# A hybrid state-space and attention step: reordered state-space stage, an early gated column, and queues and rooms at two stage borders

## The chip, the cores and the metric
The kernel runs on one core of a Trainium2 chip as one program. Its time is the device time of that program in microseconds: the median of three runs before is 2771.04 us (2769.51 to 2775.39).

## The reference
Two layers work on 1024 prompt tokens and 32 sample tokens of width 1024, all in float32. Layer 0 mixes by a diagonal state-space model with a gate, layer 1 by sparse attention over the 256 best keys; after each mixer stands a convolutional feed-forward unit of width 2816.

```python
def s5_mixer(u, ...):                       # 64 groups of 16 channels, 64 complex states each
    h = scan(a * h_prev + b @ u)            # over the tokens
    y = re(c @ h) + d * u
    z = gelu(y)
    g = z @ w_glu + b_glu                   # 1024 x 2048
    return g[:, :1024] * sigmoid(g[:, 1024:]), h_last

x = x + s5_mixer(rms_norm(x))               # layer 0
x = x + conv_ffn(rms_norm(x))
x = x + sparse_attention(rms_norm(x)) @ w_o # layer 1
x = x + conv_ffn(rms_norm(x))
```

## The kernel before
The program is a chain of stages: `ssm` (state-space model), `load_x` (the residual stream, transposed on chip), `glu` (the gate), `ffn(0)`, the projections and the index search, `attend`, the output projection, `ffn(1)`. The dense products write each float32 operand as a high and a low part, so that one product is three matmuls; a weight is loaded on SP's queue, ACT casts its high part (`whi`) and DVE subtracts to get the low part (`wlo`). Rooms in on-chip memory come from pools: a new tile waits until the room's former tile has been read. The layer that records the operations puts the instructions of each engine in order itself (by costs and readiness), so the order on an engine is not that of the code; the rows of the order below are what it made.

`ssm` cuts the 64 groups into eight octets `o` of 8 groups, and each octet into three subs `s` of 3, 3 and 2 groups. Tokens go in chunks of eight, 133 columns for a group: 128 of the prompt, then the state and four chunks of the sample. For an octet, `taps` and `maps` build the matrices `ix`, `cp`, `cps`, `tz` (DVE, with POOL's products `tt`, and DMAs of `kr` into `tz`). For a sub, `angles` makes the phases: POOL's `sel`, PE's matmul (L637), DVE's rounding `kk` (L639), PE again (L641 to L643), ACT's `cos` and `sin`. `states` multiplies the inputs by `inm` on PE, rotates them on DVE (`ga`, `gb`), copies the initial state into one column of `ga` (L671), scans (`en`, L673), and rotates back: POOL makes `pc` from `en` and `cos` (L678) while DVE makes `pq` from `en` and `sin` (L679). `outputs` sums three matmuls into `py` (L693 to L695), ACT copies it to `yo`. `rows(o)` regroups the octet's `yo` by eight DMAs on SP into `zo` (L702), applies gelu in place (L703), casts with a stride into `xh[o]` (L710), and subtracts with the same stride into `xl[o]` (L711). Final states `pcf`, `psf` are collected on POOL and stored from SP at the end.

Then `load_x` loads nine row tiles of x on ACT's queue (`xrow`, two rooms), transposes 72 blocks on PE (L236) and copies them to `xt`. `glu` goes over eight output columns `m`: 16 weight DMAs of 64 KB on SP (L152), two casts, two subtractions, then for each of three token blocks two sums over eight `k` (144 matmuls of 352 columns per column), sigmoid on ACT and the product on DVE. At the start of `attend` SP loads the first keys `kr`, values `vr` and queries `qr`; POOL splits the queries (`qp`), PE transposes them (L1292), ACT casts `q`, and the scores follow (L1308, L1309).

Of the kernel before, what the change touches and what calls it, by code (L numbers as in the profile page):

```python
# [9 lines left out]
F32 = mybir.dt.float32  # L10
# [3 lines left out]
ALU = mybir.AluOpType  # L14
# [27 lines left out]
MAGF = 12582912.0  # L42
RATE = 0.6
# [6 lines left out]
class Trunk:  # L50


    def __init__(self, tc, ctx, I, O):
# [9 lines left out]
        self.xh, self.xl = [], []  # L63

# [14 lines left out]
    def open_weights(self, ctx):  # L79
        self.open_psum(ctx)  # L80
        self.wr = ctx.enter_context(self.tc.tile_pool(name="wr", bufs=3, side="right", reuse_waits="tile"))
        self.wp = ctx.enter_context(self.tc.tile_pool(name="wp", bufs=4, side="right", reuse_waits="tile"))
# [12 lines left out]
    def load_vectors(self, pool):  # L95
# [13 lines left out]
        rows = [pool.tile([P, P], F32, tag="vrow", name="vrow", bufs=3) for _ in range(nt)]  # L109
        at = 0  # L110
        for name, s in srcs:
            self.voff[name] = at
            n, o = s.shape[0], 0
            while o < n:
                t, r = divmod(at, P)
                c = min(n - o, P - r)
                nc.sync.dma_start(rows[t][r : r + c, :], s[o : o + c, :])
                o += c
                at += c
        for t in range(nt):  # L120
# [10 lines left out]
    def weight(self, view, pool=False):  # L131
# [13 lines left out]
        return hi, lo  # L145

    def weight_rows(self, view, sh):

        nc = self.nc
        raw = self.wr.tile(sh, F32, tag="wraw", name="wraw")  # L150
        for k in range(sh[1]):
            nc.sync.dma_start(raw[:, k], view[:, :, k])  # L152
        hi = self.wp.tile(sh, F32R, tag="whi", name="whi")
        lo = self.wp.tile(sh, F32R, tag="wlo", name="wlo")
        nc.scalar.copy(hi, raw)
        nc.vector.tensor_sub(lo, raw, hi.bitcast(F32))
        return hi, lo
# [68 lines left out]
    def load_x(self, pool):  # L226
        nc, I = self.nc, self.I
        xp = I["x_prompt"].rearrange("b t d -> (b t) d")
        xs = I["x_sample"].rearrange("b t d -> (b t) d")
        for o, n in self.token_tiles():  # L230
            row = pool.tile([P, D], F32, tag="xrow", name="xrow", bufs=2)
            nc.scalar.dma_start(row[:n], xp[o : o + n] if o < TP else xs[:n])
            for h in range(2):
                ps = self.ps()
                for k in range(4):
                    nc.tensor.transpose(ps[:, k * P : k * P + n], row[:n, (4 * h + k) * P : (4 * h + k + 1) * P], self.ident[:n, :n])  # L236
                nc.any.tensor_copy(self.xt[:, 4 * h : 4 * h + 4, o : o + n], ps.rearrange("p (k t) -> p k t", t=P)[:, :, :n])
# [52 lines left out]
    def ssm_loads(self, tmp):  # L290
# [12 lines left out]
        xs = tmp.tile([TS + 8, D], F32, name="xs")  # L303
# [18 lines left out]
    def ssm_params(self, pool, tmp, ld):  # L322
# [132 lines left out]
        bst, bsw, ca, cb = (pool.tile([P, G, 16], F32, name=n) for n in ("bst", "bsw", "ca", "cb"))  # L455
# [31 lines left out]
    def ssm_input(self, tmp, ld):  # L487
# [9 lines left out]
        n = TS + 8  # L497
# [19 lines left out]
        room = [v[0:5, i : i + 1024].rearrange("c (j f) -> c j f", f=P) for v in ld["free"] for i in range(0, 3072, 1024)]  # L517
        for o in range(KD):
            t = self.xp.tile([5, 8, 8, 16], F32, tag="xh", name="um", bufs=KD)
# [10 lines left out]
    def ssm(self):  # L530

        nc, I, O = self.nc, self.I, self.O
        C = 133
        with ExitStack() as ctx:
            self.open_psum(ctx)
            pool = ctx.enter_context(self.tc.tile_pool(name="ssm", bufs=1, reuse_waits="tile"))
            with self.tc.tile_pool(name="ssmt", bufs=1, reuse_waits="tile") as tmp:
# [9 lines left out]
                pcf = pool.tile([P, 2, 64], F32, name="pcf")  # L547
                psf = pool.tile([P, 2, 64], F32, name="psf")
                tz = [pool.tile([P, 8, P], F32, name=f"tz{i}") for i in range(2)]
                m8s = [pool.tile([P, 8, C], F32, name=f"m8{i}") for i in range(2)]  # L550
                sels = [pool.tile([P, 400], F32R, name=f"sel{i}") for i in range(3)]
                zc = self._fill(tmp, "zc", [P, 1], 0.0)
                for t in tz:
                    nc.gpsimd.memset(t, 0.0)
                for t in m8s:
                    nc.gpsimd.memset(t[:, :, 0:1], 0.0)
                    nc.gpsimd.memset(t[:, :, 128:129], 0.0)
                for t in sels:
                    nc.vector.tensor_copy(t[:, 399:400], zc)
# [10 lines left out]
            W3 = lambda ng: ng * C + ng * C % 2  # L570
            flat = lambda v: v.rearrange("p g c -> p (g c)")

            def taps(o):
# [19 lines left out]
                for a, b in ((1, 128), (129, C)):  # L593
# [4 lines left out]
            def maps(o, d):  # L598
# [3 lines left out]
                kr = wk.tile([16, 8, P], F32, tag="kr", name="kr", bufs=1)  # L602
                for h in range(2):
# [21 lines left out]
            def angles(o, s):  # L625
# [12 lines left out]
                kk = wk.tile([P, 400], F32R, tag="kk", name="kk", bufs=2)  # L638
# [5 lines left out]
                cos = wk.tile([P, 3, C], F32, tag="cos", name="cos", bufs=3)[:, :ng]  # L644
                sin = wk.tile([P, 3, C], F32, tag="sin", name="sin", bufs=3)[:, :ng]
# [1040 lines left out]
```

## Time and profile before

| | us |
|---|---|
| median of three runs | 2771.04 |
| the profiled execution | 2771.09 |
| its span, first to last instruction | 2769.3 |
| PE busy in the span | 2576.5 (93%) |
| DVE / ACT / POOL busy | 1607.9 / 998.5 / 447.9 |

The profiled execution lies 0.05 us from the median, and 1.8 us of it lie outside the span. Over long stretches PE is busy without a gap, so the stages in which it is not are the ones to read: the state-space stage up to 254 us, the border behind it up to 286 us, the index search and projections, and the start and end of attention. Two views serve for that: the windows, which give the busy time of every engine in a stretch, and the waits, which name the instruction that waited and the one that released it.

### The profile page before, as it was taken

What the parts mean: (1) busy time and instruction counts of PE and PEld (TensorE: products, weight loads), DVE (VectorE), ACT (ScalarE), POOL (GpSimd) and SP (SyncE); (2) the same over time, 40 slices, a digit from 0 to 9 for tenths busy, and PEclk for the clock granted to TensorE, in tenths of its full rate; (3) what the DMA queues carried; (4) which work ended last, traced back from release to release, by engine and by line L of the source; (5) the groups of instructions that cost most, each with busy time, mean ns of one, the idle gap of its engine ahead of it and who ended that gap; (6) DMA issues with size and microseconds to landing.
All of it is one profiled execution on the core that took longest, in us unless ns stands there. A gap on an engine that the chain in (4) does not pass through costs nothing. (4 is left out here: it accounts for less than half of the span.)

```text
span 2769.3 us, 43229 instructions
## 1 busy us (share of the span) xinstructions
PE 2576.5 (93%) x17203; PEld 2466.9 (89%) x17203; DVE 1607.9 (58%) x3365; ACT 998.5 (36%) x2011; POOL 447.9 (16%) x696
## 2 busy tenths in 40 slices
PE   2887999999999999998898689999999999999999
PEld 2676999999999999997788667778999999999998
DVE  8886324644444444468799887663654444444443
ACT  4665213322222222225466577772322222222222
POOL 4673001100000000011245242220200000000000
PEclk9998999999999999998999799999999999999999
DMA  4334311111111111110111301202111111111111
GB/s 95 60 57 101 93 46 46 39 46 46 47 46 46 46 46 47 46 36 22 47 56 61 89 22 39 48 18 77 39 46 46 46 47 46 47 46 46 46 39 64
DMA packets 220662, 140.29 MB, mean 51 GB/s; under 512 B 50429, under 2 KB 212261, under 8 KB 220461
## 3 DMA queue, kind: packets, MB, share of 16 engines
q1 hardware_dynamic: 216733, 130.90, 17.3%
q10 hardware_dynamic: 3728, 6.64, 0.7%
q8 instruction: 135, 2.21, 0.3%
q14 instruction: 66, 0.54, 0.1%
HBM read 112.68 MB, written 13.40 MB: 46 GB/s over the span
## 5 line engine op out<-in xcount | busy, mean ns | idle before, releaser
L164 PE MATMUL ps_mm<-xh,whi 128*128 128x352 f32 x2688 | 870.3, 324 | 4.8 <-ACT whi L143 4.8
L166 PE MATMUL ps_mm<-xh,wlo 128*128 128x352 f32 x2688 | 869.5, 324 | 0.0
L165 PE MATMUL ps_mm<-xl,whi 128*128 128x352 f32 x2688 | 868.6, 323 | 0.0
L164 PEld LDWEIGHTS ps_mm<-xh,whi 128*128 128x128 f32 x2688 | 506.4, 188 | 5.1 <-ACT whi L143 5.0
L165 PEld LDWEIGHTS ps_mm<-xl,whi 128*128 128x128 f32 x2688 | 506.3, 188 | 0.0
L166 PEld LDWEIGHTS ps_mm<-xh,wlo 128*128 128x128 f32 x2688 | 506.0, 188 | 0.2 <-DVE wlo L144 0.2
L144 DVE TENSOR_TENSOR wlo<-wraw,whi 128x1024 fp32r<-128x1024 f32 (+1 forms) x145 | 175.4, 1221 | 416.7 <-ACT whi L143 416.7
L143 ACT CAST whi<-wraw 128x1024 fp32r<-128x1024 f32 (+1 forms) x145 | 149.9, 1047 | 711.9 <-PE ps_mm L165 701.8
L1559 DVE TENSOR_TENSOR xt<-xt,ps_mm 128x352 f32<-128x352 f32 x528 | 269.2, 519 | 191.6 <-PE ps_mm L166 191.5
L164 PE MATMUL ps_mm<-hh,whi 128*128 128x352 f32 x1056 | 341.1, 323 | 1.5 <-DVE xt L1559 1.5
L165 PE MATMUL ps_mm<-hl,whi 128*128 128x352 f32 x1056 | 340.9, 323 | 0.0
L166 PE MATMUL ps_mm<-hh,wlo 128*128 128x352 f32 x1056 | 340.6, 323 | 0.0
L1540 POOL COPY tails<-a 128x2 f32<-128x2 f32 x44 | 39.8, 904 | 1229.9 <-ACT a L1529 1229.9
L164 PEld LDWEIGHTS ps_mm<-hh,whi 128*128 128x128 f32 x1056 | 198.4, 188 | 2.1 <-DVE xt L1559 2.0
L166 PEld LDWEIGHTS ps_mm<-hh,wlo 128*128 128x128 f32 x1056 | 198.5, 188 | 0.0
L165 PEld LDWEIGHTS ps_mm<-hl,whi 128*128 128x128 f32 x1056 | 198.4, 188 | 0.0
L772 PE MATMUL ps_mm<-whi,xh 128*128 128x256 f32 (+3 forms) x560 | 163.6, 293 | 18.4 <-ACT raw L1173 18.4
L1547 DVE TENSOR_TENSOR c<-c,ps_mm 128x352 f32<-128x352 f32 (+2 forms) x176 | 71.5, 427 | 159.3 <-PE ps_mm L166 112.7
L773 PE MATMUL ps_mm<-wlo,xh 128*128 128x256 f32 (+3 forms) x560 | 161.9, 290 | 0.0
L774 PE MATMUL ps_mm<-whi,xl 128*128 128x256 f32 (+3 forms) x560 | 161.8, 290 | 0.0
L1529 ACT COPY a<-ps_mm 128x352 f32<-128x352 f32 (+2 forms) x176 | 61.9, 378 | 242.1 <-PE ps_mm L166 242.0
L772 PEld LDWEIGHTS ps_mm<-whi,xh 128*128 128x128 f32 (+1 forms) x560 | 104.1, 186 | 23.1 <-ACT raw L1173 21.6
(410 smaller groups left out, 3974.7 us busy)
## 6 DMA issues: line engine op xcount, KB each, us to landing
wraw<-in_ffn_w_up_dram SPq DMA_DIRECT2D x88, 512.0 KB
wraw<-in_ffn_w_down_dram SPq DMA_DIRECT2D x44, 512.0 KB
wraw<-in_ssm_w_glu_dram SPq DMA_DIRECT2D x128, 64.0 KB
wraw<-in_attn_w_in_dram SPq DMA_DIRECT2D x14, 512.0 KB
zo<-yo SPq DMA_DIRECT2D x64, 66.5 KB
xcm<-in_x_prompt_dram SPq DMA_DIRECT2D x8, 512.0 KB
cps<-cp SPq DMA_DIRECT2D x16, 256.0 KB
xrow<-in_x_prompt_dram ACTq DMA_DIRECT2D x8, 512.0 KB
```

What stands on the lines that cost most here:

```text
L143: nc.scalar.copy(hi, raw)
L144: nc.vector.tensor_sub(lo, raw, hi.bitcast(F32))
L164: nc.tensor.matmul(ps, wh, xh, start=(i == 0), stop=False)
L165: nc.tensor.matmul(ps, wh, xl, start=False, stop=False)
L166: nc.tensor.matmul(ps, wl, xh, start=False, stop=(i == n - 1))
L772: self.nc.tensor.matmul(ps, xh, hi[:, c, a:b], start=(k == 0), stop=False)
L773: self.nc.tensor.matmul(ps, xh, lo[:, c, a:b], start=False, stop=False)
L774: self.nc.tensor.matmul(ps, xl, hi[:, c, a:b], start=False, stop=(k == KD - 1))
L1529: nc.scalar.copy(u["a"][:, co + 2 : co + 2 + n], ps[:, to - b * BLK : to - b * BLK + n])
L1540: nc.gpsimd.tensor_copy(tails[:, u["f"], 0:2], u["a"][:, TP : TP + 2])
L1547: nc.vector.tensor_mul(h, h, bv[:, to - b * BLK : to - b * BLK + n])
L1559: nc.vector.tensor_add(self.xt[:, m, blocks[b]], self.xt[:, m, blocks[b]], ps[:, :BLK])
```

## The change
- State-space stage: a group has 134 columns, the sample's six first (state, four chunks, one pad), then the prompt's 128. `cos` and `sin` lie in one tile `cs`, `pc` and `pq` in one tile `pp`, and one multiplication on DVE fills both. The copy of the initial state into `ga` moves from DVE to ACT. `dgi` and the addition to `kr` move from DVE to POOL. `kk` has one room. `rows` writes gelu's result with the stride into `zt`, so that the cast and the subtraction run over 1056 adjacent columns; for the last octet half of the eight `zo` DMAs go to ACT's queue. The loads of the small vectors move from the start to the second octet; the final states are stored from POOL's queue.
- First gated column: the banks of `ssm` and of the dense stages are one pool. During the last octet `glu_first` loads both halves of column 0 (one on SP, one on POOL's queue) into rooms that have become free, with their casts and subtractions; the products for `k` 0 to 6 are issued behind the last outputs, those for `k` 7 behind them.
- `load_x` works on one column `m` (nine transposes) inside the first block of that column in `glu`, from `xcol`, two DMAs on SP.
- `glu` has its own weight rooms; column `m` loads column `m`'s weights in its turn (column 1 in that of column 0, its second half on POOL's queue). The first seven weight loads of `ffn(0)` stand on SP behind the `xcol` of column 6.
- Attention: the first keys' and queries' rooms and banks are ones that are free; `vr` and `rss` are issued behind the first two `qr`; the second keys are loaded two units later. For the output projection the two weight pools change places.

```diff
-        C = 133
+        C = 134
...
-                dgi = wk.tile([16, 8, 16], F32, tag="dgi", name="dgi", bufs=1)
-                nc.vector.tensor_mul(
-                    dgi, self.ident[:16, :16].rearrange("p (g q) -> p g q", g=1).to_broadcast([16, 8, 16]),
-                    par["dg"][:, gs].rearrange("p (g q) -> p g q", q=1).to_broadcast([16, 8, 16]))
-                nc.vector.tensor_add(kr[:, :, 0:16], kr[:, :, 0:16], dgi)
...
-                nc.vector.tensor_mul(ga, v3(p1), w["cos"])
-                nc.vector.tensor_mul(gb, v3(p2), w["sin"])
-                nc.vector.tensor_add(ga, ga, gb)
-                nc.vector.tensor_copy(ga[:, :, 128], smt[:, 33, w["gg"]])
...
+                nc.scalar.copy(ga[:, :, 0], smt[:, 33, w["gg"]])
+                gc = ga[:, :, 1:]
+                nc.vector.tensor_mul(gc, v3(p1)[:, :, 1:], w["cos"][:, :, 1:])
+                nc.vector.tensor_mul(gb[:, :, 1:], v3(p2)[:, :, 1:], w["sin"][:, :, 1:])
+                nc.vector.tensor_add(gc, gc, gb[:, :, 1:])
...
-                nc.gpsimd.memset(pc[:, :, 0:1], 0.0)
-                nc.gpsimd.memset(pq[:, :, 0:1], 0.0)
-                nc.gpsimd.tensor_mul(pc[:, :, 1:], en, w["cos"])
-                nc.vector.tensor_mul(pq[:, :, 1:], en, w["sin"])
-                for f, p in ((pcf, pc), (psf, pq)):
-                    nc.gpsimd.tensor_copy(f[:, :, w["gg"]].rearrange("p f g -> p g f"), p[:, :, 128:134:5])
+                pp = wk.tile([P, 2, 3, C + 1], F32, tag="pp", name="pp", bufs=2)[:, :, :ng]
+                pc, pq = pp[:, 0], pp[:, 1]
+                nc.gpsimd.memset(pp[:, :, :, 0:1], 0.0)
+                nc.vector.tensor_mul(pp[:, :, :, 1:], en.rearrange("p (s g) c -> p s g c", s=1).to_broadcast([P, 2, ng, C]), w["cs"])
+
+                nc.gpsimd.tensor_copy(fcs[:, :, :, w["gg"]].rearrange("p s f g -> p s g f"), pp[:, :, :, 5 : C + 1 : C - 5])
...
-                nc.scalar.activation(zo, zo, AF.Gelu_apprx_tanh)
...
-                    nc.scalar.copy(hi, src)
-                    nc.vector.tensor_sub(lo, src, hi.bitcast(F32))
+                    e = nc.scalar if last and i % 2 else nc.sync
+                    e.dma_start(zo[:, i, :], yo[o][16 * i : 16 * i + 16])
...
+                x = wk.tile([P, T], F32, tag="zt", name="zt", bufs=1)
+                for t0, t1, c0 in ((0, TP, 6), (TP, T, 1)):
+                    nc.scalar.activation(
+                        x[:, t0:t1].rearrange("p (c i) -> p i c", i=8), zo[:, :, c0 : c0 + (t1 - t0) // 8], AF.Gelu_apprx_tanh)
+                nc.scalar.copy(xh, x)
+                nc.vector.tensor_sub(xl, x, xh.bitcast(F32))
...
+                        if o == KD - 2:
+                            first = self.glu_first(pool, wk)
...
+                nc.gpsimd.dma_start(O["ssm_re_" + nm][0, 0], fin[64 * f : 64 * f + 64, 0:64])
+                nc.gpsimd.dma_start(O["ssm_im_" + nm][0, 0], fin[64 * f : 64 * f + 64, 64:128])
...
+        raw, hi, lo = (new(i) for i in range(3))
+        for k in range(KD):
+            (e or nc.sync).dma_start(raw[:, k], w[:, :, k, c : c + P])
+        nc.scalar.copy(hi, raw)
+        nc.vector.tensor_sub(lo, raw, hi.bitcast(F32))
+        return hi, lo
...
+        ws = [self.glu_weight(new(half), 0, half, nc.gpsimd if half else None) for half in range(2)]
+
+        def products():
+            self.first = [[self.ps()[:, :BLK] for _ in ws] for _ in range(NB)]
+            for ks in (range(KD - 1), (KD - 1,)):
+                for b in range(NB):
+                    for ps, w in zip(self.first[b], ws):
+                        self.glu_part(ps, w, b, ks)
+
+        return products
+
...
+                return self.glu_weight(tile, m, half, nc.gpsimd if m == 1 and half else None)
+
+            def residual(m):
+                raw = gp.tile([P, 9, P], F32, tag="xcol", name="xcol")
+                nc.sync.dma_start(raw[:, 0:8], xp[:, :, m * P : (m + 1) * P])
+                self.loaded = nc.sync.dma_start(raw[:TS, 8], I["x_sample"][0, :, m * P : (m + 1) * P]).ins
+                return raw
...
+                if m != 1:
+                    ws = [weight(max(m, 1), half) for half in range(2)]
+                x = residual(m)
+                if m == AHEAD:
+
+                    self.behind.append(self.loaded)
...
+                    if m:
+                        pa, pg = sums = [self.ps()[:, :BLK] for _ in ws]
+                        for ps, w in zip(sums, ws):
+                            self.glu_part(ps, w, b, range(KD))
+                    else:
+                        pa, pg = self.first[b]
+                    if b == 0:
+                        self.load_x(x, m)
...
+            if started:
+                values_in()
+            else:
+                late.append(values_in)
...
+        for tag in "sott":
+            self.ps(tag)
...
+            with self.tc.issue_after(self.loaded):
+                for f in late:
+                    f()
+                for h in range(4):
+                    nc.sync.dma_start(rss[TS * h : TS * h + TS], self.rsq[0:TS, :, 32 + h])
...
+            if a == 0:
+                last_inputs()
+            if a == 2:
+                load()
...
-            pend = [start(0), start(1)]
+            with self.tc.issue_after(self.behind.pop()) if self.behind else ExitStack():
+                pend = [start(0), start(1)]
```

PE at the end of the state-space stage, before (L693 to L695 are the last outputs, L736 and L737 the final states, L236 the transposes of x, L164 on the first gated column):

```order
L695 MATMUL ps_mm<-pq,cps 128x133
L736 MATMUL ps_aux<-ident,pcf 128x128
L737 MATMUL ps_aux<-swap,psf 128x128
L236 MATMUL ps_mm<-ident,xrow 128x128 x64
L236 MATMUL ps_mm<-ident,xrow 128x32 x8
L164 MATMUL ps_mm<-xh,whi 128x352
L165 MATMUL ps_mm<-xl,whi 128x352
L166 MATMUL ps_mm<-xh,wlo 128x352
```

The same place now (L681 to L683 outputs, L729 and L730 final states, L782 to L784 the first gated column with the weights `g`):

```order
L681 MATMUL ps_mm<-ut,tz_125 128x134
L782 MATMUL ps_mm<-xh,g_2083 128x352
L682 MATMUL ps_mm<-pp,cp 128x134
L683 MATMUL ps_mm<-pp,cps 128x134
L681 MATMUL ps_mm<-ut,tz_125 128x134
L682 MATMUL ps_mm<-pp,cp 128x134
L683 MATMUL ps_mm<-pp,cps 128x134
L729 MATMUL ps_aux<-ident,fcs 128x128
L730 MATMUL ps_aux<-swap,fcs 128x128
L783 MATMUL ps_mm<-xl,g_2083 128x352
L784 MATMUL ps_mm<-xh,g_2084 128x352
L782 MATMUL ps_mm<-xh,g_2083 128x352
```

The 72 transposes that stood between are gone from this place; they follow nine at a time inside the columns.

DVE in one sub of the state-space stage, before (`ga`, `gb`, `en`, `pq` as above; `ix` belongs to the next octet's matrices; the scan is printed as SCALAR_TENSOR_TENSOR):

```order
L639 TENSOR_SCALAR kk<-ps_mm 128x400
L668 TENSOR_TENSOR ga<-ps_mm,cos 128x399
L669 TENSOR_TENSOR gb<-ps_mm,sin 128x399
L582 TENSOR_TENSOR ix<-ix,tt 128x1024
L670 TENSOR_TENSOR ga<-ga,gb 128x399
L671 COPY ga<-smt 128x3
L673 SCALAR_TENSOR_TENSOR en<-m_127,ga 128x399
L679 TENSOR_TENSOR pq<-en,sin 128x3x133
```

And now:

```order
L628 TENSOR_SCALAR kk<-ps_mm 128x402
L667 TENSOR_TENSOR pp<-en,cs 128x6x134
L659 TENSOR_TENSOR ga<-ps_mm,cs 128x3x133
L660 TENSOR_TENSOR gb<-ps_mm,cs 128x3x133
L571 TENSOR_TENSOR ix<-ix,tt 128x1024
L661 TENSOR_TENSOR ga<-ga,gb 128x3x133
L663 SCALAR_TENSOR_TENSOR en<-m_127,ga 128x402
L667 TENSOR_TENSOR pp<-en,cs 128x6x134
```

The copy into `ga` is gone, `pp` stands for `pq` with twice the columns, and `kk` stands ahead of it.

SP at the start of attention, before:

```order
L1268 DMA kr<-kd 128x8x64 x2
L1271 DMA vr<-vd 128x8x64
L1287 DMA qr<-qd 128x256
L1271 DMA vr<-vd 128x8x64
L1392 DMA rss<-rsq 32x4x1
L1268 DMA kr<-kd 128x8x64 x2
L1392 DMA rss<-rsq 32x4x1 x3
L1287 DMA qr<-qd 128x256 x2
L1268 DMA kr<-in_cache_k_dram 128x8x64
```

And now:

```order
L1343 DMA kr<-kd 128x8x64 x2
L1369 DMA qr<-qd 128x256 x2
L1348 DMA vr<-vd 128x8x64
L1483 DMA rss<-rsq 32x4x1 x4
L1369 DMA qr<-qd 128x256
L1343 DMA kr<-kd 128x8x64 x2
L1348 DMA vr<-vd 128x8x64
L1369 DMA qr<-qd 128x256 x2
L1343 DMA kr<-in_cache_k_dram 128x8x64
```

The two first `qr` stand ahead of the first `vr` now, and the second `kr` behind a third `qr`.

## Rows read from the trace of the kernel before

**Rows 1.** Windows: length, busy us per engine (instructions), clock, DMA share, GB/s.
```profile
core 0: us, PE busy (x) PEld busy (x) DVE busy (x) ACT busy (x) POOL busy (x), PEclk, DMA share, GB/s
60.00:254.00 194.00, 157.62 (x1046) 133.70 (x1047) 168.68 (x233) 122.06 (x230) 120.71 (x169) 0.95 0.30 55
254.00:286.00 32.00, 15.91 (x76) 13.03 (x74) 15.48 (x23) 9.87 (x13) 0.00 (x0) 0.58 0.66 198
...
300.00:460.00 160.00, 160.00 (x998) 160.00 (x997) 41.40 (x59) 29.05 (x43) 1.89 (x2) 1.00 0.19 53
...
1564.00:1580.00 16.00, 2.47 (x12) 2.07 (x12) 9.03 (x26) 7.70 (x19) 1.13 (x2) 0.57 0.69 183
1580.00:1600.00 20.00, 13.14 (x68) 10.77 (x67) 12.88 (x47) 10.07 (x27) 6.90 (x11) 0.58 0.31 74
```

**Rows 2.** Waits of PE in 60 to 254 us: total, times, longest.
```profile
PE ps_mm L642 <- DVE kk L639: 22.3, 13, 3.2
PE ps_mm L693 <- DVE ga L668: 5.1, 6, 1.4
PE ps_mm L694 <- POOL pc L678: 4.7, 5, 2.1
```

**Rows 3.** Lines of DVE by form, 60 to 254 us: busy, mean ns; idle before.
```profile
L679 DVE TENSOR_TENSOR pq<-en,sin 128x399 f32<-128x399 f32 x16 | 16.4, 1028 | 0.5
...
L711 DVE TENSOR_TENSOR xl<-zo,xh 128x1024 fp32r<-128x1024 f32 x6 | 13.0, 2168 | 0.3 <-issue 0.2
L671 DVE COPY ga<-smt 128x3 f32<-128x3 f32 x16 | 12.6, 788 | 0.4
...
L582 DVE TENSOR_TENSOR ix<-ix,tt 128x1024 f32<-128x1024 f32 x8 | 9.7, 1218 | 4.4 <-POOL tt L580 4.4
...
L612 DVE TENSOR_TENSOR kr<-kr,dgi 16x128 f32<-16x128 f32 x8 | 7.3, 908 | 0.3 <-DMA cps<-cp 0.3
```

**Rows 4.** The same view of POOL.
```profile
L678 POOL TENSOR_TENSOR pc<-en,cos 128x399 f32<-128x399 f32 x16 | 24.3, 1517 | 24.4 <-DVE en L673 21.2 <-ACT sin L649 3.2
...
L580 POOL TENSOR_TENSOR tt<-smt,bsw 128x1024 f32<-128x1024 f32 x8 | 17.5, 2182 | 1.3 <-DVE cp L588 1.3
```

**Rows 5.** Lines of PE by form, 254 to 312 us.
```profile
L236 PE MATMUL ps_mm<-ident,xrow 128*128 128x128 f32 x64 | 14.8, 413 | 15.8 <-DMA xrow<-in_x_prompt_dram 15.8
```

**Rows 6.** Timelines of PE, ACT, SP there: start, length, instruction, idle before.
```profile
253.96 0.39 PE L737 MATMUL ps_aux<-swap,psf 128*128 128x128 f32 x2
...
286.18 0.66 PE L164 MATMUL ps_mm<-xh,whi 128*128 128x352 f32 x1
...
252.18 1.28 ACT L703 ACT_TABLE_LOAD   x1 [3.40 <-DMA zo<-yo]
...
267.61 1.09 ACT L703 ACTIVATE zo<-zo 128x1064 f32<-128x1064 f32 x1 [7.93 <-DMA zo<-yo]
...
244.79 19.11 SPq L702 DMA_DIRECT2D zo<-yo  x16
...
267.50 37.91 SPq L152 DMA_DIRECT2D wraw<-in_ssm_w_glu_dram  x50
```

**Rows 7.** Timeline at the start of attention.
```profile
1570.13 0.37 ACTq L1180 DMA_DIRECT2D vd<-raw  x1
...
1574.33 1.07 ACT L820 CAST kh<-ps_t 128x512 fp32r<-128x512 f32 x2 [1.04 <-issue]
...
1575.05 0.57 SPq L1287 DMA_DIRECT2D qr<-qd  x1
...
1578.23 0.41 POOL L1158 TENSOR_SCALAR qp<-qr 128x256 fp32r<-128x256 f32 x1 [15.23 <-DMA qr<-qd]
...
1580.92 0.48 PE L1308 MATMUL ps_s<-kh,q 128*128 128x128 f32 x1 [0.68 <-ACT q L1294]
...
1587.12 0.91 POOL L1146 TENSOR_TENSOR ms<-ms 128x384 bf16<-128x384 bf16 x1 [7.68 <-DVE ms L1145]
...
1591.28 0.58 PE L1308 MATMUL ps_s<-kh,q 128*128 128x256 f32 x1 [0.68 <-ACT q L1294]
```

More of the change, by code (lines that the diff above doesn't have):

```diff
@@ L63, in __init__ @@
         self.xh, self.xl = [], []
+        self.behind = []
     def open_dense(self, ctx):
@@ L108, in load_vectors @@
         self.voff = {}
-        rows = [pool.tile([P, P], F32, tag="vrow", name="vrow", bufs=3) for _ in range(nt)]
+        rows = pool.tile([P, 8, P], F32, tag="kr", name="vrow", bufs=1)
         at = 0
@@ L224, in token_tiles, with load_x @@
         return [(o, min(P, T - o)) for o in range(0, T, P)]
[L226 to L237, printed above, removed]
+    def load_x(self, raw, m):
+        nc = self.nc
+        for t0 in range(0, 9, 4):
+            ps = self.ps("aux")
+            n = min(4, 9 - t0) * P if t0 < 8 else TS
+            for t in range(t0, min(t0 + 4, 9)):
+                c = P if t < 8 else TS
+                nc.tensor.transpose(ps[:, (t - t0) * P : (t - t0) * P + c], raw[:c, t], self.ident[:c, :c])
+            nc.any.tensor_copy(self.xt[:, m, t0 * P : t0 * P + n], ps[:, :n])
     def store_block(self, pool, b):
@@ new lines, in ssm @@
+            nc.tensor.matmul(ps[:, :P], fcs[:, 1].rearrange("p f g -> p (f g)"), swap, start=False, stop=True)
+            fin = wk.tile([P, P], F32, tag="dgi", name="fin", bufs=1)
+            nc.vector.tensor_copy(fin, ps[:, :P])
+            for f, nm in enumerate(("sample", "prompt")):
+                nc.gpsimd.dma_start(O["ssm_re_" + nm][0, 0], fin[64 * f : 64 * f + 64, 0:64])
+                nc.gpsimd.dma_start(O["ssm_im_" + nm][0, 0], fin[64 * f : 64 * f + 64, 64:128])
+            rows(KD - 1)
@@ L745, in glu, with glu_part @@
+    def glu_part(self, ps, w, b, ks):
+        nc = self.nc
+        hi, lo = w
+        sl = slice(b * BLK, (b + 1) * BLK)
+        for k in ks:
+            xh, xl = self.xh[k][:, sl], self.xl[k][:, sl]
+            nc.tensor.matmul(ps, hi[:, k], xh, start=(k == 0), stop=False)
+            nc.tensor.matmul(ps, hi[:, k], xl, start=False, stop=False)
+            nc.tensor.matmul(ps, lo[:, k], xh, start=False, stop=(k == KD - 1))
     def glu(self, after_block):
         nc, I = self.nc, self.I
-        w = I["ssm_w_glu"][0].rearrange("(k g q) f -> q g k f", g=8, q=16)
+        xp = I["x_prompt"][0].rearrange("(t p) f -> p t f", p=P)
@@ L752, in glu @@
                 for b in range(NB):
                     sl = slice(b * BLK, (b + 1) * BLK)
-                    pa, pg = self.ps(), self.ps()
-                    for ps, (hi, lo) in ((pa, wa), (pg, wg)):
-                        self.product(ps[:, :BLK], [(hi[:, k], lo[:, k], self.xh[k][:, sl], self.xl[k][:, sl]) for k in range(KD)])
+                    if m:
[4 more added lines that the diff above has]
+                        pa, pg = self.first[b]
@@ L1255, in attend @@
         nc.vector.tensor_copy(identr, self.ident)
+        for tag, shape, bufs, dt in (
+            ("kh", [P, T], 2, F32R), ("kl", [P, T], 2, F32R), ("vr", [P, 9, 64], 2, F32), ("q", [P, 512], 2, F32R),
+            ("kr", [P, 9, 2, 64], 1, F32), ("qr", [P, 4, 64], 2, F32), ("qp", [P, 4, 2, 64], QPB, F32R)):
+            kp.tile(shape, dt, tag=tag, name=tag, bufs=bufs)
+        late, started = [], []
         def keys(g, sample):
@@ L1388, in attend, with last_inputs @@
         qops = {steps[0]: queries(*steps[0])}
-        load()
         rss = ap.tile([P, 4], F32, name="rss")
-        for h in range(4):
-            nc.sync.dma_start(rss[TS * h : TS * h + TS], self.rsq[0:TS, :, 32 + h])
+        def last_inputs():
+            with self.tc.issue_after(self.loaded):
[3 more added lines that the diff above has]
+                    nc.sync.dma_start(rss[TS * h : TS * h + TS], self.rsq[0:TS, :, 32 + h])
+            started.append(True)
         live = {}
```

147 lines of the change are left out of this document (76 added, 71 removed).

## The prediction
> **What bounds the kernel now.** I read three views, in this order. The windows first: in 300 to 460 us PE is busy 160.00 of 160.00 us, and the same holds for the feed-forward units, so time can only come from the stretches in which PE waits [rows 1]. The change touches three of them. In the state-space stage (60 to 254 us) PE is busy 157.6 of 194 us and DVE 168.7, the highest share of any engine; at the border behind it (254 to 286) PE is busy 15.9 of 32 at a granted clock of 0.58; at the start of attention (1564 to 1600) 15.6 of 36 at 0.57 and 0.58 [rows 1]. Then the waits, for who ends them: in the state-space stage PE waits 22.3 us for DVE's `kk`, 5.1 us for DVE's `ga` and 4.7 us for POOL's `pc`, together 32.1 of its 36.4 idle microseconds [rows 2]. DVE itself is idle for 25 us of the 194, so what PE waits for is its turn in DVE's queue. Last the timelines of the two borders, for the chain that ends each [rows 6, 7].
>
> **Border to the gate, before.** The last matmul of the state-space stage ends at 253.96 + 0.39 = 254.35 and the first gated matmul starts at 286.18: 31.8 us [rows 6]. Two chains fill them side by side: 72 transposes that wait 15.8 us for rows of x [rows 5], and SP's queue, on which the gate's weights start at 267.50 behind the two last sets of `zo` [rows 6].
>
> **Now.** The weights of column 0 are loaded inside the stage and the transposes are taken apart. Behind the last output PE has 126 products of column 0 (three blocks, two halves, seven `k`, three parts). A product of 352 columns costs 160.00 / 998 = 0.160 us [rows 1], so they last 20.2 us, and 18 more follow for the last `k`. What that needs: `xl` of octet 6, and, 20 us later, of octet 7. In before ACT's gelu of octet 7 starts at 267.61, 13.3 us behind the last output [rows 6]; the strided work behind it now falls to gelu, and cast and subtraction run over adjacent columns, so its `xl` comes some 5 us later, at about 18 us: covered, with 2 us to spare, and more since half of its DMAs go to ACT's queue. Octet 6 is tighter: its eight DMAs start at 244.79, ACT gets them at 252.18 and works until about 258 [rows 6]; PE needs it at the 19th product, 2.9 us behind 254.4. I put 1 us of wait there. At the border of columns 0 and 1, ACT has two sigmoids ahead of the two casts for column 1, and DVE's subtraction stands behind these (about 1.2 us, as the 1024-column operation of [rows 3]): 2 us.
>
> The transposes do not go away. In before 64 of them took 14.8 us, 0.231 each, at a clock of 0.58 [rows 1, 5]; at the full clock that is 0.134 (an estimate), so 72 cost 9.6 us inside columns in which PE has no gap. Gain: 31.8 - 9.6 - 3 = 19 us. Bounds: 12 if the two waits are 5 us each, 24 if transposes slip into gaps that are there anyway.
>
> **State-space stage.** Off DVE: the copy of three columns into `ga`, 16 x 788 ns = 12.6 us, and the eight two-group copies, some 4 by proportion; the addition to `kr`, 7.3; in `xl`, 13.0 for six octets becomes 6 x 1.218 x 1056/1024 = 7.5 at the rate of the 1024-column operation, 5.5 less [rows 3]. `pp` has 804 columns where `pq` had 399; at the same rate that is 0.96 us against 1.03, so it costs nothing more [rows 3]. Together 29 us of 168.7. POOL loses `pc`, 24.3 us and about 8 for the narrow ones [rows 4], and takes the 7.3 of `kr` and the small `dgi`; it is busy 120.7 of 194 [rows 1], so this fits. ACT takes 24 copies; at DVE's 788 ns they would be 19 us on an engine that is busy 122 of 194 [rows 1, 3], and they stand ahead of the scan, so I cost them at nothing; if ACT were late, a scan would wait for it instead.
>
> How much of DVE's 29 us reaches the end? PE's waits for `kk` are 13 in 24 subs, 3.2 us at most [rows 2]. DVE saves 29/24 = 1.2 us a sub, and `kk` now stands ahead of `pp`: 13 x 1.2 = 16 us. Five waits for `pc` shrink by 1.52 - 0.96 = 0.56 us each [rows 2 to 4], 3 us. Against that stand column 0's two casts and two subtractions in the last octet (2 x 1.2 us on DVE) and the eight POOL DMAs, which stand ahead of the next `m8`, `sel` and `pp`'s zeros; 19 - 2.4 - 5 = 12 us. Bounds: 5 us of loss if nothing but the additions counts, 29 of gain if all of DVE's saving does. The value lies nearer to the waits' row than to either end.
>
> The trace of before has no DMA issued from POOL. From below its price is that of SP's own issue of the same 64 KB pieces, 37.91/50 = 0.76 us [rows 6], from above POOL's long operations, 2.18 us [rows 4]. POOL's idle time in an octet is (194 - 120.7 + 32 - 9)/8 = 12 us, so eight DMAs stay hidden at 0.76 (6 us) and stand out by 5 at 2.18; I take 5 of this above, for the order in which they lie.
> The Trainium skill speaks against this part: "SBUF — State Buffer" (section "SBUF: two separate sides") says that a DMA issued from the GpSimd queue cannot get its descriptors written while DVE runs a copy or cast in its two-port mode, and "DMA: Bandwidth & Descriptors" (section "Anatomy of one DMA") gives about 2.0 us of fixed cost for such a DMA. By the second figure eight of them would stand out by 8 x 2.0 - 12 = 4 us, and the sum would stay where it is; no run here shows either yet.
>
> **Attention.** Before, the first `qr` leaves SP at 1575.05, behind a `vr` that waits for ACT's last stores of `vd`, and POOL has it at 1578.23, 3.2 us later; scores start at 1580.92 [rows 7]. Now `qr` stands ahead of `vr`, but its place in the queues still waits for the store issued at 1570.13 [rows 7]. With the same 3.2 us for that store it leaves at about 1573.3: 2 us earlier. The keys' casts on ACT at 1574.33 [rows 7] do not move and come next. The second unit's scores start at 1591.28, because POOL's second split lay behind the mask operation that POOL began at 1587.12 after 7.68 us of waiting [rows 7]; now three splits lie ahead of the mask, and the second unit can follow the first directly. In 1580 to 1600 PE is idle 6.9 us and DVE 7.1 [rows 1]; I take 5. Together 7 us; bounds 0 (DVE is late at the next unit and takes all back) and 3 + 7 = 10.
>
> **The rest.** At the output projection the first weight still waits for the last product of attention, so the pools' change of place is put at nothing. The early loads for `ffn(0)` are put at nothing too: PE is full there. Vector loads and final states leave queues in which nothing waits behind them.
>
> **Sum.** 19 + 12 + 7 = 38 us off the profiled execution's 2771.09 (span 2769.3 and 1.8 outside); that execution is at the median, 2771.04. 2771 - 38 = 2733 us. About 0.2%, 5.5 us, is what a measurement of this kernel can tell from no change.
>
> **Rivals.**
> 1. The state-space stage keeps its length: PE's waits are latency, not DVE's load. For it: PE alone is busy 157.6 of 194, and every sub is a chain over four engines. Against it: DVE is the busiest. 2771 - 19 - 7 = 2745.
> 2. All of DVE's saving reaches the end and the borders go well: 2771 - 29 - 22 - 8 = 2712. For it: 32.1 us of waits on DVE and POOL [rows 2].
> 3. The gate's columns get a wait each: transposes share two banks, whose copies lie on ACT and DVE behind casts. With the 3 us of the first border at each of seven: 2771 - 38 + 21 = 2754. Against it: in 300 to 460 ACT is busy 29 and DVE 41 of 160 [rows 1].
> 4. Slower than before: POOL's queue becomes the bound. Eight DMAs of p us each stand ahead of the last octet's work (cover 12 us), and twelve ahead of column 1's second half (cover 23 us of column 0, less 4 for landing and casts). It eats 8p - 12 + 12p - 19 = 20p - 31 us, of which 5 are in the sum already: 44 more are needed to be slower by 0.2%, so it decides from p = 4.0 us. At 4.5 us: 2771 - 38 + 54 = 2787. Against it: the nearest rows are 0.76 and 2.18 us [rows 4, 6].
> The Trainium skill's rule on starved descriptors, named above, is the one by which p could grow so far.
>
> **How the numbers follow.** Forecast 0.44 (its own range 2722 to 2742), rival 1 0.24, rival 2 0.13, rival 3 0.10, rival 4 0.05, and 0.04 that several gains fail and the time stays. Faster by over 0.2%: 0.44 + 0.24 + 0.13 + 0.10 = 0.91; same 0.04; slower 0.05. The range takes in rivals 1 to 3, each with a few microseconds about its value, and leaves out rival 4: 2706 to 2760.
>
> **What would show it.** Right: PE goes from the last output to products of column 0 with a gap under 2 us; nine transposes in each column and no wait over 3 us at a column's border; the waits for `kk` fall from 22.3 to about 10 us and the octets' period shortens; the second unit's scores follow the first within 3 us. Wrong: PE waits for `sel`, `pp` or column 1's weights behind POOL's DMAs; `kk` waits unchanged; the 7 us at attention coming back as DVE's work in the units that follow.

## The result, and the profile after

The changed kernel takes 2752.45 us (median of four runs, 2749.19 to 2755.65) against 2771.08 for the kernel before: a ratio of 0.993, interval 0.9912 to 0.9949. That is 18.6 us faster, inside the range (2706 to 2760), and half of the 38 us that were forecast. Run again beside other experiments it came out the same: 2752.73 us, ratio 0.9933 (0.9918 to 0.9947).

The profiled execution of the changed kernel, the longest of the four, took 2755.65 us, 15.4 less (by span) than that of before. The windows show that the stretches have moved by different amounts. Columns as in [rows 1]; the state-space stage now ends at 256.86, so its window is 60 to 257:

```profile
60.00:257.00 197.00, 163.40 (x1051) 137.70 (x1051) 158.78 (x189) 125.91 (x255) 100.87 (x121) 0.92 0.31 60
257.00:260.00 3.00, 2.60 (x17) 2.31 (x15) 0.00 (x0) 2.96 (x4) 0.00 (x0) 1.00 0.00 0
260.00:280.00 20.00, 18.43 (x113) 18.20 (x114) 2.74 (x5) 4.70 (x6) 6.38 (x12) 1.00 0.57 146
300.00:460.00 160.00, 157.98 (x992) 155.50 (x991) 52.73 (x93) 42.76 (x78) 7.96 (x8) 1.00 0.26 74
1560.00:1576.00 16.00, 7.82 (x37) 7.12 (x38) 8.37 (x36) 8.05 (x21) 3.81 (x7) 0.50 0.75 193
1576.00:1596.00 20.00, 17.26 (x143) 13.00 (x143) 16.11 (x57) 16.85 (x51) 10.41 (x18) 0.94 0.21 55
```

The border behind the stage is gone: where PE was busy 15.9 of 32 us at a clock of 0.58 [rows 1], it now works at full clock. But the stage has not become shorter. DVE is busy 158.8 us where it was 168.7, 10 less and not 29, and the granted clock of PE fell from 0.95 to 0.92, so PE's own work takes longer (163.4 us, 157.6 before). Taken apart by the ends of the stretches in both timelines:

| stretch | forecast | found |
|---|---|---|
| state-space stage, last matmul 254.35 to 256.86 | -12 | +2.5 |
| border and gate, first part of the gate's last product 475.5 to 461.4 | -19 | -16.5 |
| start of attention, first scores and the next unit | -7 | -5.4 |
| all else (border to `ffn(0)` +1.3, projections and index +2.1, remainder) | 0 | +4.0 |
| sum | -38 | -15.4 |

So 14.5 of the 22.6 missing microseconds are in one stretch, the state-space stage. PE's waits there (total, times, longest) answer [rows 2]:

```profile
PE ps_aux L608 <- ACT kr L600: 9.3, 5, 4.1
PE ps_aux L599 <- DVE cp L577: 7.8, 6, 3.3
PE ps_mm L631 <- DVE kk L628: 5.4, 6, 2.2
PE ps_mm L682 <- DVE pp L667: 5.4, 4, 3.1
```

The waits for `kk` fell from 22.3 to 5.4 us, further than forecast. In their place stand a wait that was not there before, for ACT's `kr`, and one for DVE's `cp`, which was 1.5 us. The waits of ACT itself say why `kr` is late:

```profile
ACT ga L657 <- DVE en L663: 21.8, 10, 5.3
ACT cs L635 <- PE ps_mm L632: 21.3, 10, 4.3
```

Ten times ACT stands still, 21.8 us in all, before the little copy into `ga` that was moved to it. One such place in the timeline (start, length, engine, instruction, idle before; all engines, other rows left out):

```profile
158.70 2.28 POOL L574 TENSOR_TENSOR tt<-smt,cb 128x1024 f32<-128x1024 f32 x1 [1.31 <-DVE ix L571]
159.21 2.63 DVE L663 TENSOR_TENSOR_SCAN en<-m,ga 128x402 f32<-128x402 f32 x1
...
161.88 0.20 ACT L657 COPY ga<-smt 128x3 f32<-128x3 f32 x1 [3.13 <-DVE en L663]
161.88 1.00 DVE L667 TENSOR_TENSOR pp<-en,cs 128x804 f32<-128x804 f32 x1
162.19 1.05 ACT L600 COPY kr<-ps_aux 16x512 f32<-16x512 f32 x2
162.82 1.57 PEld L608 LDWEIGHTS ps_aux<-ident,ix 128*128 128x128 f32 x8 [4.27 <-ACT kr L600]
162.82 1.97 PE L608 MATMUL ps_aux<-ident,ix 128*128 128x128 f32 x8 [4.07 <-ACT kr L600]
```

The copy is for a later sub. It writes into a room of `ga` that an earlier scan still reads, so it waits for the end of that scan; behind it in ACT's queue stand the two copies of `kr`, whose products have long been done, and PE waits 4.07 us for them. The same lines show a second thing. The scan takes 2.63 us, while POOL's multiply `tt` started half a microsecond ahead of it. By lines (busy, mean ns):

```profile
L663 DVE TENSOR_TENSOR_SCAN en<-m,ga 128x402 f32<-128x402 f32 x16 | 24.1, 1506 | 1.1 <-ACT ga L657 0.3
L667 DVE TENSOR_TENSOR pp<-en,cs 128x804 f32<-128x804 f32 x15 | 19.9, 1327 | 0.4
...
L700 DVE TENSOR_TENSOR xl<-zt,xh 128x1056 fp32r<-128x1056 f32 x6 | 10.1, 1685 | 1.3 <-ACT xh L699 1.3
```

The scan's line in the kernel before:

```profile
L673 DVE TENSOR_TENSOR_SCAN en<-m,ga 128x399 f32<-128x399 f32 x16 | 16.0, 1000 | 0.5
```

Alone, a scan of 402 columns still takes 0.98 to 1.00 us in the changed kernel; five that had `tt` started half a microsecond ahead of them take 2.63 to 2.65. `pp` is 1.00 us in the row at 161.88 and 1.33 on average.

### The profile page after: what moved, and what is told of

Its sections match the earlier page's. It is cut to its first block, busy times and chain, and to the rows that moved or that the text cites. A ratio compares the mean times of both kernels' runs of the same rounds, so it can differ in the third digit from the quotient of the medians.

```text
span 2753.9 us, 43113 instructions
## 1 busy us (share of the span) xinstructions
PE 2576.4 (94%) x17203; PEld 2464.9 (90%) x17203; DVE 1584.6 (58%) x3300; ACT 1006.8 (37%) x2054; POOL 434.5 (16%) x659
## 5 line engine op out<-in xcount | busy, mean ns | idle before, releaser
L160 PE MATMUL ps_mm<-xh,whi 128*128 128x352 f32 x2304 | 746.7, 324 | 4.9 <-ACT whi L151 4.9
L162 PE MATMUL ps_mm<-xh,wlo 128*128 128x352 f32 x2304 | 746.0, 324 | 0.0
L161 PE MATMUL ps_mm<-xl,whi 128*128 128x352 f32 x2304 | 745.0, 323 | 0.0
L160 PEld LDWEIGHTS ps_mm<-xh,whi 128*128 128x128 f32 x2304 | 434.5, 189 | 5.1 <-ACT whi L151 5.1
L161 PEld LDWEIGHTS ps_mm<-xl,whi 128*128 128x128 f32 x2304 | 434.5, 189 | 0.0
L162 PEld LDWEIGHTS ps_mm<-xh,wlo 128*128 128x128 f32 x2304 | 434.3, 188 | 0.2 <-DVE wlo L152 0.2
## 6 DMA issues: line engine op xcount, KB each, us to landing
cps<-cp SPq DMA_DIRECT2D x16, 256.0 KB
```

What stands on the lines that cost most here:

```text
L160: nc.tensor.matmul(ps, wh, xh, start=(i == 0), stop=False)
L161: nc.tensor.matmul(ps, wh, xl, start=False, stop=False)
L162: nc.tensor.matmul(ps, wl, xh, start=False, stop=(i == n - 1))
```

## The experiments

A in the expectations is the theory that the small copy in ACT's in-order queue lost the stage's gain; B is the rival, that DVE decides: its amount of work, and the scans that run long there. Every run is measured against the kernel before on the same chip. "Last output" is the start of the stage's last output product: 253.5 in the kernel before, 256.0 in the changed one, 255.1 when that was run again, so single profiles of one kernel differ by about 1 us there.

**The copy back on DVE.**
```diff
-                nc.scalar.copy(ga[:, :, 0], smt[:, 33, w["gg"]])
+                nc.vector.tensor_copy(ga[:, :, 0], smt[:, 33, w["gg"]])
```


> The changed kernel with the copy of the initial state into ga back on DVE. Theory A (in ACT's queue the copy waits for the scan that still reads its room, 21.8 us in all, and kr, ut and yo wait behind it): PE's 9.3 us of waits for ACT's kr go away, the last output of the state-space stage comes at about 248 us instead of 256.9, the whole at about 2744 us. Theory B (DVE's operations grow beside POOL's, so any work given back to DVE lengthens the stage): the copies cost DVE 5 to 16 us again, the last output at 258 to 265 us. Theory C (PE itself bounds the stage): within 2 us of 256.9.

2749.03 us, ratio 0.9908 (0.9893 to 0.9923). Last output at 249.2, 6 to 7 us sooner, with 12 us more work on DVE. PE's waits in 60 to 250 us:

```profile
PE ps_mm L631 <- DVE kk L628: 12.1, 11, 2.2
PE ps_aux L599 <- DVE cp L577: 9.6, 6, 3.4
...
PE ps_aux L608 <- ACT kr L600: 1.4, 3, 0.6
```
The wait for `kr` is all but gone; a part of it returns as a wait for `kk` (12.1 us, 5.4 before this edit), since DVE has the copies again. The whole run's interval overlaps that of the changed kernel, and its time is 5 us above the 2744 of the expectation; the stage's end does not leave a doubt. In the stage A holds.

**A third room for `ga`** (and one fewer for `en`, which pays for it).
```diff
-name="ga", bufs=2)
+name="ga", bufs=3)
```


> The changed kernel with three rooms for ga (and one for en, which DVE alone writes and reads); the copy stays on ACT. Theory A: the copy waits for a scan one sub earlier, so ACT's wait of 21.8 us falls below 5, PE's waits for kr go, the last output at 246 to 249 us, the whole at about 2743 us. Theory B and theory C: within 2 us of 256.9.

2755.56 us, 0.9934 (0.9919 to 0.9949), last output 255.3: no change, so A's forecast of 246 to 249 missed. ACT still waits 23.0 us for the scans: with a room more, the copy was put one sub earlier in the order and waits for the same scan. So it is the place in the queue and not the number of rooms.

**The diagonal's multiply and add of `kr` on DVE instead of POOL.**
```diff
-                nc.gpsimd.tensor_mul(
+                nc.vector.tensor_mul(
                     dgi, ...
-                nc.gpsimd.tensor_add(kr[:, :, 0:16], kr[:, :, 0:16], dgi)
+                nc.vector.tensor_add(kr[:, :, 0:16], kr[:, :, 0:16], dgi)
```


> The changed kernel with dgi and the addition to kr back on DVE. Theory B: DVE takes 5 to 9 us more, POOL 15 us less, scan and pp get shorter (1.5 and 1.3 us now); the last output between 3 us earlier and 3 later. Theory A: the tz DMAs start earlier or later by a microsecond, no change of the stage beyond 2 us. Theory C: the same.

2751.23 us, 0.9916 (0.9901 to 0.9931), last output 254.2, the wait for `kr` at 9.1 as before. Alone it is worth 1 to 2 us at most, within what single profiles differ by.

**`pc` on POOL again.**
```diff
-                nc.vector.tensor_mul(pp[:, :, :, 1:], en.rearrange(...).to_broadcast([P, 2, ng, C]), w["cs"])
+                nc.gpsimd.tensor_mul(pc[:, :, 1:], en, w["cos"])
+                nc.vector.tensor_mul(pq[:, :, 1:], en, w["sin"])
```


> The changed kernel with the pc half of pp back on POOL (DVE makes pq alone). Theory B: the scan's mean falls from 1.5 to about 1.1 us because POOL waits for it again, but pc takes 1.5 us on POOL: last output 0 to 4 us later than 256.9. Theory A: PE's waits for pc return (5 us) and those for kr stay: last output 3 to 6 us later. Theory C: within 2 us.

2752.73 us, 0.9922 (0.9906 to 0.9939), last output 259.1, 3 to 4 us later. The move of `pc` off POOL was a gain in the stage. The scan's mean stayed at 1.48 us (402 columns), so `pc` on POOL alone does not keep `tt` away from the scans; this part of B missed. One of four such places in this run, with `pc` back on POOL:

```profile
186.63 2.30 POOL L574 TENSOR_TENSOR tt<-smt,cb 128x1024 f32<-128x1024 f32 x1 [1.16 <-DVE ix L571]
187.14 2.64 DVE L663 TENSOR_TENSOR_SCAN en<-m,ga 128x402 f32<-128x402 f32 x1
```

**The state added by TensorE, no copy at all.** In this run and the next, column 0 of the products also takes in the first sample tokens, which belong elsewhere.
```diff
-    nc.tensor.matmul(p1[:, g * C : (g + 1) * C], inm[:, 0:P], ut[:, g], start=True, stop=True)
+    nc.tensor.matmul(p1[:, g * C : (g + 1) * C], inm[:, 0:P], ut[:, g], start=(g == 0), stop=False)
...
-    nc.scalar.copy(ga[:, :, 0], smt[:, 33, w["gg"]])
+    nc.tensor.matmul(v3(p1)[:, :, 0], self.ident, smt[:, 33, w["gg"]], start=False, stop=True)
```


> The changed kernel with neither copy: PE adds the initial state into its column of p1 (one small matmul a sub), and the three operations on ga and gb run over all columns. Theory A (the copy in ACT's queue held up kr, ut and yo): the last output of the state-space stage at most at 249 us, as with the copy on DVE (249.2). Theory B (DVE's load counts as well): DVE is rid of the 12 us that the copies cost it there, the last output at 243 to 246 us, the whole 4 us under that run. Theory C (PE): 24 more matmuls cost 2 to 3 us, the last output at 250 to 252.

2753.18 us (2748.16 to 2756.03), 0.993 (0.9913 to 0.9946), last output 249.5. In the stage it is the run with the copy on DVE over again, though DVE is busy 158.9 us in 60 to 250 instead of 168.2. B, read as DVE's amount of work, fails: 9 us off DVE bought nothing. The whole run kept less of it than the stage shows; the gate's last product stands at 456.8 (455.5 with the copy on DVE).

**That, with the diagonal on DVE.**


> The same, and dgi and the addition to kr on DVE. Theory B: 5 us more on DVE against 15 less on POOL: within 2 us of the run without it. Theory A: kr's way to tz is shorter by POOL's 1.3 us operations: 1 to 2 us earlier, as the run with kr on DVE alone was.

2746.81 us, 0.9911 (0.9896 to 0.9926), last output 248.1, gate's last product 451.7. In the stage that is 1.3 us sooner than without it, which both theories allow.

**Attention started as before** (the rooms, banks and late loads at its start taken out, the rest as changed; `load()` back ahead of the units):
```diff
-            if a == 0:
-                last_inputs()
-            if a == 2:
-                load()
```


> The changed kernel with the start of attention as in the kernel before (rooms, banks, order of the first loads). If that part of the change is worth what its border shows (first scores 2.2 us, steady state 5.2 us better against the stage before it): 4 to 6 us slower than the changed kernel. If later units take it back: within 2 us.

2757.79 us, 0.9951 (0.9937 to 0.9966), beside **the changed kernel again** in the same call:

> The changed kernel unaltered, for the comparison on one chip: 0.993 of the kernel before; last output of the state-space stage at 256 to 257 us, last product of the gate at 461 us.

2752.73 us. The attention part is worth 5.1 us by the medians of these two; their profiled executions, which reach attention at the same time, differ by 3.4 (spans 2753.5 and 2750.1). The intervals just overlap.

**The copy and the diagonal both on DVE** (the first and the third edit together).


> The changed kernel with the copy of the initial state on VectorE again (24 copies of [128 x ng]) and the diagonal's multiply and add of each octet (16 instructions of 16 partitions) on VectorE too. Theory A (the loss sat in instructions that stand in the in-order queues of ScalarE and POOL ahead of what TensorE waits for): both moves add up, the last output product of the state-space stage comes 1 to 3 us ahead of the 249.2 of the run with the copy alone, TensorE's waits for kr stay at 1 to 2 us, and the ratio is .988 to .991. Theory B (VectorE's load decides the stage): 7 us more of work on VectorE beside the changed kernel, 4 us beside the run with the copy alone, so the stage ends at 252 or later and the ratio is .992 or more.

2744.35 us (2742.43 to 2745.55), ratio 0.9896 (0.988 to 0.9913): the fastest version that computes all of it, 10 us below the changed kernel by the ratios (0.0037 x 2771), and its interval lies clear of the 0.9918 to 0.9947 of the second run of that. In the stage only 250.3, so the expected 1 to 3 us beyond the first edit did not show there; the gate's last product is at 453.0, 2.5 sooner than with the copy alone.

**The state by TensorE with the group's products over columns 1 to 133.**
```diff
-    nc.tensor.matmul(p1[:, g * C : (g + 1) * C], inm[:, 0:P], ut[:, g], start=(g == 0), stop=False)
+    nc.tensor.matmul(p1[:, g * C + 1 : (g + 1) * C], inm[:, 0:P], ut[:, g, 1:], start=(g == 0), stop=False)
```


> The state is added by TensorE as in x5 and x6, now with the products of each group over columns 1 to 133 alone, so that column 0 holds the initial state and nothing else; the diagonal's two instructions stand on VectorE. Theory A: as x6, last output product at 247 to 250, ratio .990 to .992; the shorter products change nothing that can be seen. Theory B (VectorE's load decides): 8 us less on VectorE than x9_ga_and_kr_on_dve, so 5 us or more ahead of that run in the stage.

2747.18 us, 0.9909 (0.9893 to 0.9925), last output 247.9: 2.4 ahead of the run before it, not 5, and no faster as a whole. DVE is busy 160.8 us in 60 to 250 instead of 168.2, and again its amount of work is not it.

**Without the second state product.**
```diff
-    nc.tensor.matmul(oy, d["cps"][:, g0 + g]..., w["pq"][:, g, 0:C], start=False, stop=True)
```


> x9_ga_and_kr_on_dve without the third product of each group's output (cps by pq, 64 groups, 128 matmul instructions, 25.9 us busy in the run with the copy on VectorE); one of the two state terms is left out of the output by this, and all else, the pq half of the product on VectorE and the cps transfers too, stays. Theory C (TensorE's own work bounds the stage once the waits on ScalarE are gone): the stage ends 18 to 26 us sooner than in x9, near 225, and the ratio is .981 to .985. Theory D (the round through the four engines, not TensorE's work, sets an octet's period): the stage ends less than 10 us sooner, TensorE's waits for kk, cp and pp grow by what its products lost, and the ratio is .987 or more.

2749.67 us, 0.9912 (0.9897 to 0.9926); the last output product starts at 248.4. The 25.9 us of the expectation are the sum of a line whose matmuls overlap their neighbours; the starts of these products lie 0.23 us apart, so about 15 us of PE's time are gone (64 x 0.23, an estimate). The stage is at most 2 us shorter. C falls even so: 15 us less would have put the end near 235. D holds for the stage's end and the ratio, but not in its last part: the waits for `kk`, `cp` and `pp` hardly grew (29.1 to 29.4 us together). Windows of 60 to 250 us, first of the run with both edits, then of this one:

```profile
60.00:250.00 190.00, 154.91 (x1042) 130.35 (x1042) 168.17 (x229) 123.25 (x232) 86.47 (x105) 0.96 0.32 62
```
```profile
60.00:250.00 190.00, 149.68 (x929) 123.25 (x929) 166.76 (x230) 123.25 (x232) 88.85 (x105) 0.93 0.32 62
```
PE has 113 instructions fewer in the window and is busy only 5.2 us less: the granted clock fell from 0.96 to 0.93, and the ones left take longer (the first output product 305 ns in the mean, 299 before). PE is not the bound here, though its busy share hardly shows it.

**Without POOL's multiplies beside the scans** (from the run with both edits). Only the first multiply is left; its result stands in for all the others, so the tables that it goes into are wrong.
```diff
-    tt = wk.tile([P, 8, 8, 16], F32, tag="tt", name="tt", bufs=1)
-    nc.gpsimd.tensor_mul(tt, bc(smt[:, 8:16, gs]), bg(par["bsw"][:, gs]))
+    if o == 0:
+        tt0.append(wk.tile([P, 8, 8, 16], F32, tag="tt", name="tt", bufs=1))
+        nc.gpsimd.tensor_mul(tt0[0], bc(smt[:, 8:16, gs]), bg(par["bsw"][:, gs]))
+    tt = tt0[0]
...
-    tt = wk.tile([P, 8, 8, 16], F32, tag="tt", name="tt", bufs=1)
-    nc.gpsimd.tensor_mul(tt, bc(smt[:, 24:32, gs]), bg(par["cb"][:, gs]))
```


> x9_ga_and_kr_on_dve with the two multiplies tt of each octet on POOL (16 of [128 x 1024], 39.3 us there) left out but for the first, whose result serves all octets, so the coefficient tables of the state-space stage are wrong by this; VectorE's instructions are all there. No tt can then run beside a scan: the scan's mean falls from 1.45 to about 1.0 us under either theory, and VectorE has 11 us less to do in the stage. Theory E (the scan that is slow beside POOL's multiply is what the stage waits for): the last state product comes 8 us or more ahead of the 246.8 of x9_ga_and_kr_on_dve, near 237, and the ratio is .985 to .9875. Theory D (the round through the four engines takes it back, as with the 12 us that x5 took off VectorE): 4 us or less ahead, ratio .988 to .991, with longer waits elsewhere or more half-clock time.

2727.23 us (2725.92 to 2727.53), ratio 0.9833 (0.9817 to 0.985): 17 us below the run with both edits, last output at 228.9, 21 us sooner. The scan's lines, first with both edits, then here:

```profile
L663 DVE TENSOR_TENSOR_SCAN en<-m,ga 128x402 f32<-128x402 f32 x16 | 27.5, 1722 | 0.4
```
```profile
L665 DVE TENSOR_TENSOR_SCAN en<-m,ga 128x402 f32<-128x402 f32 x16 | 18.0, 1125 | 0.4
```
and this run's window, with PE's largest waits in it:
```profile
60.00:250.00 190.00, 166.14 (x1153) 142.95 (x1153) 153.16 (x234) 130.92 (x240) 58.41 (x102) 0.99 0.36 74
```
```profile
PE ps_aux L601 <- DVE cp L579: 7.9, 7, 2.9
PE ps_mm L633 <- DVE kk L630: 4.1, 5, 1.5
```
The waits for `kk` were 19.0 us in the run with both edits. The scans give back 10.6 us with the narrow ones (34.9 to 24.3), DVE's waits for `tt` 2.9, and the clock is higher: this window runs 21 us into the gate, but in 60 to 229, all of it the stage, the clock is 1.00, and it was 0.97 there with both edits. E's forecast is passed by far, and D, which was nearer in the run before, is wrong here; whether the scans alone did it is taken up below. (The 246.8 in this expectation was read a few products ahead of the last one, which starts at 250.3.)

## Why the prediction was right and where it failed

**Direction and range** came from the two borders, and these were read rightly: 16.5 and 5.4 us together would give 2749. The forecast's own range, 2722 to 2742, was missed. The wide one held because it took in rivals 1 and 3 (2745 and 2754); so part of that is the width, not the reading of the state-space stage.

The gate: PE was to go from the last output to column 0 without a gap. It does, and column 0's first product is even put in ahead of the stage's end (254.29, where [rows 6] had 286.18):

```profile
254.29 0.41 PE L782 MATMUL ps_mm<-xh,g 128*128 128x352 f32 x1
...
260.70 0.43 PE L782 MATMUL ps_mm<-xh,g 128*128 128x352 f32 x1 [1.10 <-ACT xh L699]
...
261.99 0.43 PE L783 MATMUL ps_mm<-xl,g 128*128 128x352 f32 x1 [0.87 <-DVE xl L700]
...
283.81 0.43 PE L782 MATMUL ps_mm<-xh,gw 128*128 128x352 f32 x1 [1.42 <-ACT gw L749]
284.08 1.03 PE L230 MATMUL ps_aux<-ident,xcol 128*128 128x128 f32 x8
```
The two waits for octet 6 are 2.0 us together (1 was forecast), the one at the border of columns 0 and 1 is 1.4 (2 was forecast). Eight transposes take 1.03 us, 0.129 each, where the estimate was 0.134; with the ninth and its copy a column pays about 1.3 us and not 1.2. The term of 19 was sized within 2.5 us, rival 3 (3 us at every column) did not come.

**Attention**: 5.4 between the traces of before and after (5.1 by the medians of the experiment, 3.4 by its traces) for 7, inside its bounds. The second unit now follows the first, as predicted: 2.8 us after the first scores, where it was 10.4 (1580.92 to 1591.28 [rows 7]):

```profile
1568.09 0.47 PE L1390 MATMUL ps_s<-kh,q 128*128 128x128 f32 x1 [0.67 <-ACT q L1376]
...
1570.89 0.52 PE L1390 MATMUL ps_s<-kh,q 128*128 128x256 f32 x1
```

**The step that failed** is in the state-space stage: "ACT takes 24 copies; [...] they stand ahead of the scan, so I cost them at nothing; if ACT were late, a scan would wait for it instead." The busy time was no issue: 0.2 us a copy, less than the 0.79 that were allowed. What was not asked is what the copy itself waits for, and who is queued behind it. Its room is free only when an earlier scan ends; that wait was on DVE too, where it costs nothing, since a scan and a copy on one engine come one after the other anyway. On ACT it became a wait of up to 5.3 us, ahead of `kr` of up to 3.6, and PE waited up to 4.1 us for `kr`. Taking the copy back gives 6 to 7 of the 14.5 us.

**The second size that was off** is DVE's saving, 29 us; 10 were found. Its largest term is the copy itself, 16 x 788 ns = 12.6 us. That mean hides two kinds of copy. Ten of the 16 took 0.15 to 0.17 us. Five took 1.88 to 1.90, each beside a `tt` that POOL had begun about half a microsecond earlier, and one took 1.51 beside another `tt`. One of the five, in the kernel before:

```profile
182.81 2.37 POOL L585 TENSOR_TENSOR tt<-smt,cb 128x1024 f32<-128x1024 f32 x1
183.31 1.90 DVE L671 COPY ga<-smt 128x3 f32<-128x3 f32 x1
185.24 0.99 DVE L673 TENSOR_TENSOR_SCAN en<-m,ga 128x399 f32<-128x399 f32 x1
```
The copy ends with `tt`, and the scan behind it runs with nothing of POOL beside it (0.99 us). In the changed kernel (the rows at 158.70 and 159.21) DVE's next instruction at this place is the scan, and it meets `tt` in the copy's stead: five scans of 2.63 to 2.65 us for five copies of 1.9. The scans grew by 8.1 us (16.0 to 24.1), so most of the 12.6 was not saved but moved. It was not `pc` that kept the two apart, as the run with `pc` back on POOL shows. Nor does the copy's return to DVE bring its cover back: with both edits the copies stand at other places in the order, none between the start of such a `tt` and the scan, and six scans take 2.70 to 2.72. Two smaller terms: `pp` takes 1.33 us instead of 0.96, and `xl` 1.69 instead of 1.26. Leaving POOL's multiplies out took 21 us off the stage in the version with both edits.

**Rivals.** Rival 1, the stage keeps its length (2745 us), comes nearest. For its reason speak the two runs that took 7 to 9 us off DVE and moved the stage's end by 2.4 at most; against it, that its waits are not latency alone, speak the 6 to 7 us of the copy and the 21 of POOL's multiplies. Rival 2 (2712, all of DVE's saving reaches the end) did not come. Rival 4 is refuted: POOL issues a DMA in 0.57 us, below both bounds (0.76 and 2.18) and far from the 4.0 from which it would have decided:

```profile
L748 POOL DMA_DIRECT2D g<-in_ssm_w_glu_dram x8 | 4.4, 571 | 0.0
```
The Trainium skill's caution about such DMAs ("SBUF — State Buffer", "SBUF: two separate sides") was named beside it: in these rows the eight are issued back to back, and no product of column 0 waits for its weights; when their descriptors were written no run here shows.

**What is open.** Taking the copies off DVE (9 us) changed nothing, taking POOL's multiplies out (18 us off DVE up to each stage's end, 37 off POOL) changed 21. The last run also freed POOL's queue, and the order on DVE moved with it (`cp` no longer waits for `tt`), so how much is the longer scan and how much POOL's own lateness was not taken apart. A version that keeps the multiplies and holds them away from the scans was not tried. The 4.0 us lost behind the gate were not looked into by an experiment.

## What to carry to other kernels

Before moving a small instruction to an engine with time to spare, ask what it waits for and who stands behind it in that queue: a 0.2 us copy cost 6 us because it had to wait for its room. A duration read in the trace holds beside the neighbours that it had there: a mean of 788 ns was mostly copies of 1.9 us beside another engine and copies of 0.17 us by themselves. Before such a term is counted as saved, see which instruction will stand in that place next. In this stage, which PE did not bound, removing its work lowered its granted clock (0.96 to 0.93), and its busy share said little.

## What was not expected of the hardware

- A scan of [128 x 402] on DVE takes 0.98 to 1.00 us by itself, 2.63 to 2.72 when a multiply of [128 x 1024] on POOL began about half a microsecond ahead of it; it then ends about 0.86 us behind that multiply, as if it had waited for nearly all of it. A copy of [128 x 3] took 1.88 to 1.90 there instead of 0.15 to 0.17. When the scan began first and the multiply 0.16 us later, the scan kept its 0.98 and the multiply took 2.65 us; with nothing on DVE beside it one took 2.01. In these rows the one that comes second pays most. Beside POOL's multiply of [128 x 402], begun ahead of it, the scan took 1.24 to 1.53.
- A multiply of [16 x 128] took 1.34 us on POOL on average, 0.28 to 0.36 on DVE; a copy of [128 x 3] took 0.2 us on ACT.
